# Residual scale and bias as a task beside the gated unit, interleaved GELU, two gates placed anew

## The chip, the cores and the metric

One core of a Trainium2 chip runs the whole program. TensorE (PE) multiplies matrices into PSUM, VectorE (DVE), ScalarE (ACT) and GpSimd (POOL) work on elements, and SyncE (SP) issues every DMA of the kernel in one queue. The engines run side by side, each in its own fixed order, and wait for one another through semaphores. The metric is the device time of one execution in microseconds (us).

## The reference

A decoder trunk of two layers over 528 tokens (16 meta tokens and 512) and 1024 channels. Each layer projects the normalised stream `h`, runs three causal mixers on it (S5, Mamba-2 SSD, gated DeltaNet), merges them with sigmoid gates, projects once more and normalises:

```python
proj = h @ w_in[layer]
# S5 branch, after its scan
v = jax.nn.gelu(y)
v = v * jax.nn.sigmoid(v @ w_glu + b_glu)
y_a = v * jax.nn.silu(z)
...
# merge of the branches and the end of a layer
outs = jnp.einsum('btnw,nwd->btnd', branches, w_branch[layer])
gates = jax.nn.sigmoid(gate_logits.reshape(bsz, t, N_BRANCH, D_MODEL) + b_gate[layer])
merged = jnp.sum(gates * outs, axis=2)
h = _layer_norm(ALPHA * h + merged @ w_out[layer], ln_g[layer], ln_b[layer])
```

## The kernel before

**Products.** All large products are made in float32 precision from two parts. A weight tile `wr` comes by DMA (four buffers), ACT rounds 128 x 256 of it into `wh`, and DVE or POOL computes the rest, `wl = wr - wh`. Such a split of a weight feeds twelve matmuls on PE: three products (`hTh,wh`, `hTl,wh`, `hTh,wl`), two blocks of 128 rows of the weight, two blocks of 264 tokens. `pj` is the PSUM tile of a product, in two buffers.

**Order.** A layer is a list of items that run one after the other: `Gemm` (a product), `Start` (start a task), `Need` (finish a task first), `Back` (read a kept gate back), `OutProj`, and a few more. Smaller work is written as tasks, Python generators, of which `pump()` runs the next piece whenever a product has passed a split. When a piece may run is decided while the program is built, by a planner: the class `Clock` keeps a modelled time for each engine, for every buffer's last write and read, and for the DMA queue. A bare `yield` lets the task go on when its inputs are done by the model, `yield LEAD` somewhat earlier than the model's end of the last operation. `tte` gives an operation to DVE or POOL, whichever is done earlier by the model. So a change of a cost in `Clock` alters the order of instructions on all engines, and nothing else. On the chip each engine then keeps the order that was fixed.

**The places in a layer.** After the S5, SSD and DeltaNet tasks and the merge of branch 2 (`merge_all(2, ...)`) the task `v` applies the GELU to S5's output in two halves: `yc` is loaded from DRAM (`dys`, written with another layout), `gl` is the tanh argument, `vhi` and `vlo` the two parts of the result. Meanwhile PE does the kept gates (`KEPT`: products of gates of branch 0, done early, stored to DRAM in `dgate`) and the merge of branch 1. `Need v` stands before the six GLU products (`w_glu`, about 707 to 736 us in layer 0, 1545 to 1572 in layer 1), then come the six products for S5's gate path z (to 773 and 1606), then the merge of branch 0 (to 811 and 1643), whose gates come back through `Back` (`gth<-dgate`), and then the output projection in four quarters of 256 columns (`OutProj`, to 876 and 1697). In layer 0 the task `s5p1`, the S5 parameters of layer 1 (tiles `s5t`, `s5f`), is started before the GLU products too.

**The residual.** `hdram[l]` holds the normalised stream before its scale and bias. `o_pre` loads its tiles of 128 tokens into `zt` (and the rows of scale and bias into `res`); each quarter of `OutProj` multiplies and adds these for its 256 columns, adds the products (`wo` in PSUM) and takes the statistics (`lnst`) for the next norm. The 16-token tile of layer 0 takes a path of its own (`few_products`).

**The inversion.** DeltaNet's triangular systems are solved in blocks: DVE forms `UL` by products `pr`, `UL` goes to DRAM (`dU`) and comes back transposed (`Ub`), DVE transposes it into `tb`, and PE multiplies (`y<-tb,N`). There are four such places, two for each layer.

## Time and profile before

| What | Value |
| --- | --- |
| Runs (us) | 1722.65, 1719.12, 1711.24; median 1719.12 |
| Profiled execution (us) | 1713.22 |
| Its span in the trace (us) | 1711.5 |
| PE busy | 1619.9 us, 95% |
| DVE busy | 1302.4 us, 76% |
| ACT busy | 821.2 us, 48% |
| POOL busy | 196.4 us, 11% |

The span is the time from the first to the last recorded instruction of the profiled execution. Busy times are sums over the span, so an engine with 76% may be full in one stage and idle in another. All instructions carry line 229, the helper that issues them, so they are told apart by tiles: `wl<-wr,wh` is the operation that reads `wr` and `wh` and writes `wl`.

### The profile page before, as it was taken

To read this page: it belongs to the slowest core of one execution; us is meant where nothing else is said; L and a number is where in the kernel's file an instruction comes from. 1 tells how busy PE (TensorE), PEld (TensorE's weight loads), DVE (VectorE), ACT (ScalarE), POOL (GpSimd) and SP (SyncE) were. 2 spreads that over 40 slices of the span, in tenths; PEclk is the share of its full clock that TensorE was granted. 3 is DMA by queue.
4 is the path that set the end of the run, shared out by engine and by line. 5 is a ranking of instruction groups with operands and counts; after the bars stand their busy time and mean duration, and the time that the engine had idled before them with its cause. 6 is when DMAs were issued, how large, how long until landed. Compare 5 with 4: busy or idle time off the path is not lost.

```text
span 1711.5 us, 40925 instructions
## 1 busy us (share of the span) xinstructions
PE 1619.9 (95%) x15583; PEld 1546.9 (90%) x15583; DVE 1302.4 (76%) x3413; ACT 821.2 (48%) x2057; POOL 196.4 (11%) x352
## 2 busy tenths in 40 slices
PE   6899999999999999999889999999999999999996
PEld 5889999998889899999789999999989999999986
DVE  6897879779868775775767686888888687756676
ACT  5356554347834343443155655444566344344432
POOL 4000000201001000001530000002001000000043
PEclk9999999999999999999999998999999999999998
DMA  5223322252245234336232233232512453443551
GB/s 180 71 81 91 99 72 54 95 115 61 58 105 119 78 114 119 101 92 203 65 119 87 76 98 90 60 85 82 108 54 64 129 103 99 119 130 97 159 168 69
DMA packets 160149, 169.72 MB, mean 99 GB/s; under 512 B 67344, under 2 KB 98192, under 8 KB 159952
## 3 DMA queue, kind: packets, MB, share of 16 engines
q1 hardware_dynamic: 159952, 167.10, 35.1%
q8 instruction: 123, 2.02, 0.5%
q14 instruction: 74, 0.61, 0.1%
HBM read 144.40 MB, written 22.64 MB: 98 GB/s over the span
## 4 chain that ended last, share of the span: by engine, by line
PE 72%; DVE 15%; DMA 6%; issue 3%; ACT 2%; SPq 2%; POOL 0%; DVEq 0%; POOLq 0%; ACTq 0%
PE pj L229 52%; PE wo L229 4%; DVE wl L229 3%; PE y L229 2%; SPq L229 2%; DMA dU<-UL 2%; PE Y L229 2%; PE seg L229 1%; PE o L229 1%; DVE s5t L229 1%; DMA gth<-dgate 1%; DVE pr L229 1%; DVE zt L229 1%; DMA yc<-dys 1%; PE z L229 1%
## 5 line engine op out<-in xcount | busy, mean ns | idle before, releaser
L229 PE MATMUL pj<-hTh,wh 128*128 128x264 f32 (+1 forms) x2432 | 521.8, 295 | 2.0 <-ACT wh L229 2.0
L229 PE MATMUL pj<-hTh,wl 128*128 128x264 f32 (+1 forms) x2432 | 498.6, 285 | 11.4 <-DVE wl L229 11.1
L229 PE MATMUL pj<-hTl,wh 128*128 128x264 f32 (+1 forms) x2432 | 498.6, 286 | 0.0
L229 ACT ACTIVATE wh<-wr 128x256 fp32r<-128x256 f32 x820 | 325.5, 413 | 265.5 <-PE pj L229 214.1
L229 DVE TENSOR_TENSOR wl<-wr,wh 128x256 fp32r<-128x256 f32 x749 | 315.1, 435 | 168.1 <-ACT wh L229 161.5
L229 PEld LDWEIGHTS pj<-hTh,wl 128*128 128x128 f32 x2432 | 380.5, 190 | 15.7 <-DVE wl L229 15.4
L229 PEld LDWEIGHTS pj<-hTh,wh 128*128 128x128 f32 x2432 | 379.0, 191 | 9.4 <-issue 3.5
L229 PEld LDWEIGHTS pj<-hTl,wh 128*128 128x128 f32 x2432 | 382.0, 190 | 0.0
L229 POOL TENSOR_TENSOR wl<-wr,wh 128x256 fp32r<-128x256 f32 x71 | 62.0, 874 | 882.6 <-ACT wh L229 714.2
L229 PE MATMUL pj<-yhi,wh 128*128 128x264 f32 (+1 forms) x576 | 120.2, 290 | 11.9 <-ACT wh L229 5.6
L229 PE MATMUL pj<-yhi,wl 128*128 128x264 f32 (+1 forms) x576 | 117.5, 286 | 3.4 <-DVE wl L229 3.4
L229 PE MATMUL pj<-ylo,wh 128*128 128x264 f32 (+1 forms) x576 | 117.5, 286 | 0.3 <-DVE ylo L229 0.3
L229 PEld LDWEIGHTS pj<-yhi,wh 128*128 128x128 f32 x576 | 90.0, 192 | 14.4 <-issue 6.0
L229 PEld LDWEIGHTS pj<-yhi,wl 128*128 128x128 f32 x576 | 90.2, 191 | 3.9 <-DVE wl L229 3.9
L229 PEld LDWEIGHTS pj<-ylo,wh 128*128 128x128 f32 x576 | 90.6, 192 | 0.8 <-DVE ylo L229 0.8
L229 ACT ACTIVATE craw<-pj 128x528 f32<-128x528 f32 x56 | 34.0, 607 | 54.6 <-PE pj L229 37.3
L229 PE MATMUL wo<-wo,mhi 128*128 128x256 f32 x256 | 51.8, 298 | 2.4 <-DVE wo L229 1.9
L229 ACT ACTIVATE segr<-triu,sc_ghi 128x128 fp32r<-128x128 f32 (+1 forms) x168 | 52.3, 375 | 2.9 <-PE sS L229 2.8
L229 ACT ACTIVATE segr<-triu,sc_glo 128x128 fp32r<-128x128 f32 (+1 forms) x168 | 52.2, 374 | 0.0
L229 ACT ACTIVATE gth<-pj,pars 128x528 f32<-128x528 f32 (+1 forms) x48 | 33.0, 688 | 28.4 <-PE pj L229 28.4
L229 PEld LDWEIGHTS wo<-wo,mhi 128*128 128x128 f32 x256 | 42.2, 201 | 4.9 <-DVE wo L229 2.9
L229 DVE TENSOR_TENSOR s5w<-s5w,s5w 128x132 f32<-128x132 f32 (+1 forms) x144 | 43.1, 313 | 2.9
(384 smaller groups left out, 2776.4 us busy)
## 6 DMA issues: line engine op xcount, KB each, us to landing
wr<-in_w_main_dram SPq DMA_DIRECT2D x304, 256.0 KB
wr<-in_w_branch_dram SPq DMA_DIRECT2D x48, 256.0 KB
wr<-in_w_out_dram SPq DMA_DIRECT2D x32, 256.0 KB
s5t<-dK SPq DMA_DIRECT2D x192, 32.0 KB
wr<-in_w_branch_dram SPq DMA_DIRECT2D x48, 128.0 KB
zt<-hdram SPq DMA_DIRECT2D x8, 512.0 KB
dus<-us SPq DMA_DIRECT2D x12, 264.0 KB
ub<-dus SPq DMA_DIRECT2D x32, 99.0 KB
```

Of the source, the lines that this page charges most:

```text
L229: r = f(*args, **kw)
```

## The change

1. `Clock`: a DMA whose contiguous run is under 256 bytes ends 1900 ns after its bytes have moved by the model, before 650. This concerns the small DMAs of the inversion.
2. `head_scalars` and `s5_bc` get two and three more points at which other work may be put between their operations (`yield LEAD`).
3. `s5_gelu` takes both halves in one task: both `yc` loads are issued first, and the first part of a row's work (square to tanh) runs ahead of the second part of the row before. The tanh rows use the buffers `craw`.
4. The gate of (0,0) is read back ahead of the last z product, and of the last four kept gates one, (0,1), is made after the merge of branch 1.
5. The residual's scale and bias become a task `residual`, started after `Need v`: it loads a tile of `hdram` into `zr` (two buffers `nu`), does the multiplication and the addition in two halves of 512 columns, and stores it back; `OutProj` loads the finished tile. `Need res` stands before `o_pre`. In the order that results, all 20 operations of layer 0 and 16 of layer 1 are on DVE.

```diff
--- before.py
+++ after.py
@@ -193,7 +193,7 @@
             for s in out.shape:
                 size *= s
             self.moved = max(self.q + 650, self.moved) + size / (360.0 if run >= 512 else 180.0)
-            end = self.moved + 650
+            end = self.moved + (1900 if run < 256 else 650)
         else:
             end = t + self.cost(e, op, out, ins, kw)
             self.t[e] = end
@@ -743,8 +743,10 @@
         act(eg, ac[:, :, 0:6], AF.Exp)
         dt8 = small([P, NC, 12], "sc_dt", bufs=1)
         ts(V, dt8, u[:, :, 6:18], 0.125, MUL)
+        yield LEAD
         ts(V, beta, beta, 1.0, ADD)
         V.reciprocal(out=beta, in_=beta)
+        yield LEAD
         glo = small(sh, "sc_glo", bufs=1)
         tt(V, glo, g, f32(ghi), SUB)
         hs.update(dt8=dt8, beta=beta, g=(f32(ghi), glo), te=te, et=et, eg=eg)
@@ -1446,10 +1448,13 @@
         u = t2("su")
         tte(y, b, kk("kr"), MUL)
         tte(u, bx, kk("kis"), MUL)
+        yield LEAD
         tte(y, y, u, ADD)
         tte(yx, bx, kk("krs"), MUL)
+        yield LEAD
         tte(b, b, kk("ki"), MUL)
         tte(yx, yx, b, SUB)
+        yield LEAD
         ts(V, c[64:128], c[64:128], -1.0, MUL)
         w["b"] = dict(y=y, yx=yx, c=c, cx=cx)
         yield
@@ -1580,23 +1585,37 @@
             DMA.dma_start(out=dst[:, :, 7 - i, :], in_=ys[16 * i:16 * i + 16])
         st["yd"] = d
 
-    def s5_gelu(st):
-
-        yc = big("yc")
-        DMA.dma_start(out=yc, in_=st["yd"].rearrange("(a g) c i n -> (g c) a (i n)", a=3))
-        hi, lo = st["v"] = (big("vhi", F32R), big("vlo", F32R))
-        yield
-        for i in range(3):
-            x = yc[:, i, :]
-            t = row("gl")
+    def s5_gelu(sts):
+
+        ycs = [big("yc") for _ in sts]
+        for st, yc in zip(sts, ycs):
+            DMA.dma_start(out=yc, in_=st["yd"].rearrange("(a g) c i n -> (g c) a (i n)", a=3))
+        yield
+
+        def first(x):
+            t = rot(sp, [P, T + 3], F32, "craw", "gl", 2)[:, 0:T]
             act(t, x, AF.Square)
             ts(V, t, t, 0.044715, MUL, 1.0, ADD)
             tte(t, t, x, MUL)
             act(t, t, AF.Tanh, scale=GELU_C)
-            yield
+            return t
+
+        def second(x, t, hi, lo, i):
             stt(x, t, 1.0, x, ADD, MUL)
             hilo_row(x, hi, lo, i, 0)
-            yield
+
+        left = None
+        for st, yc in zip(sts, ycs):
+            for i in range(3):
+                t = first(yc[:, i, :])
+                yield LEAD
+                if left:
+                    second(*left)
+                    yield LEAD
+                if i == 0:
+                    st["v"] = (big("vhi", F32R), big("vlo", F32R))
+                left = (yc[:, i, :], t, *st["v"], i)
+        second(*left)
 
 
     lnc = const([P, DEPTH, 2 * KD], F32, "lnc")
@@ -1828,6 +1847,8 @@
             g, o = zip(*[merge(n, d, xs) for d in range(d0, d1)])
 
             def gate_item(d):
+                if (n, d0 + d) == (0, 0):
+                    return
                 if (n, d0 + d) in kept:
                     items.append(Back(KEPT.index((n, d0 + d))))
                 else:
@@ -1885,12 +1906,32 @@
                 zt[c] = nu("zt") if c < 2 else tok_tile("zt")
                 DMA.dma_start(out=zt[c][:n], in_=hdram[l][t0:t0 + n, :])
                 zt["st", c] = small([P, 4, 6], "lnst", bufs=5)
-            if 0 in which:
-                zt["in"] = [row_vec(A["ln_in" + k] if l == 0 else A["ln" + k][l - 1:l, :],
-                                    flat(sp.tile([P, 2, T], F32, tag="bc", name=nm("res"), bufs=2))[:, 0:D])
-                            for k in ("_g", "_b")]
-            elif lastl:
+            if lastl and 0 not in which:
                 zt["gb"], zt["bb"] = (row_vec(A[k][l:l + 1, :], tok_tile(k)) for k in ("ln_g", "ln_b"))
+
+        def residual():
+
+            rows = [row_vec(A["ln_in" + k] if l == 0 else A["ln" + k][l - 1:l, :],
+                            flat(sp.tile([P, 2, T], F32, tag="bc", name=nm("res"), bufs=2))[:, 0:D])
+                    for k in ("_g", "_b")]
+            zs = {}
+
+            def load(c):
+                t0, n = cs[c]
+                zs[c] = nu("zr")
+                DMA.dma_start(out=zs[c][:n], in_=hdram[l][t0:t0 + n, :])
+
+            load(0)
+            for c in cs:
+                t0, n = cs[c]
+                if c + 1 < len(cs):
+                    load(c + 1)
+                yield
+                for x, op in zip(rows, (MUL, ADD)):
+                    for h in (slice(0, 512), slice(512, D)):
+                        tte(zs[c][:n, h], zs[c][:n, h], x[:n, h], op)
+                        yield LEAD
+                DMA.dma_start(out=hdram[l][t0:t0 + n, :], in_=zs[c][:n])
 
         def last(c):
             return lambda: last_task(zt[c], *cs[c], zt["st", c], zt["gb"], zt["bb"])
@@ -1954,14 +1995,11 @@
                     products(1, range(KD - 1))
                 for c in seq:
                     t0, n = cs[c]
-
-                    zh = zt[c][:n, 256 * qn:256 * qn + 256]
-                    for x, op in zip(zt["in"], (MUL, ADD)):
-                        tte(zh, zh, x[:n, 256 * qn:256 * qn + 256], op)
                     if n < 32:
                         few_products(c)
                     else:
                         products(c, range(KD - 1 if qn == 0 and c < 2 else 0, KD))
+                    zh = zt[c][:n, 256 * qn:256 * qn + 256]
                     stt(zh, zh, ALPHA, ps[c][:n], MUL, ADD)
                     if n < 32:
                         for i in (32, 64, 96):
@@ -2028,22 +2066,23 @@
         items.append(Start("sp" + L, lambda: ssd_post(l, hs, sd, to)))
         merge_all(2, xc, 6, 8)
         items.append(Mark("xc" + L))
-        def f_v():
-            for hf in range(2):
-                yield from s5_gelu(s5[hf])
-
-        items.append(Start("v" + L, f_v, "fB" + L, "sp" + L))
+        items.append(Start("v" + L, lambda: s5_gelu(s5), "fB" + L, "sp" + L))
+        keep_gates(3)
+        merge_all(1, xb, 0, 8, "sp" + L)
+
         keep_gates(len(KEPT) - len(kept))
-        merge_all(1, xb, 0, 8, "sp" + L)
-
         items.append(Need("v" + L))
+        items.append(Start("res" + L, residual))
         if not lastl:
             items.append(Start(f"s5p{l + 1}", lambda: s5_params(l + 1)))
         for o in range(6):
             items.append(Gemm(A["w_glu"][l, o], 6, vx, FULL, c_glu(o)))
         items.append(Do(lambda: None))
         for o in range(6):
+            if o == 5:
+                items.append(Back(KEPT.index((0, 0))))
             main(CT_ZA + o, c_za(o), blocks)
+        items.append(Need("res" + L))
         items.append(Do(lambda: o_pre((0, 1))))
         merge_all(0, xa, 0, 8)
         items.append(Do(lambda: None))
```

Three places show how the order of instructions moves. DVE's order in the first inversion of layer 0, before, up to the transpose `tb` (`x` and `g_r` are other work of the same task):

```order
L229 TENSOR_TENSOR wl_3028<-wr_2732,wh_3027 128x256
L229 TENSOR_TENSOR g_rt_3009<-g_r_3008 128x30
L229 SCALAR_TENSOR_TENSOR g_rt_3009<-g_rt_3009,g_x_2710 128x30
L229 SCALAR_TENSOR_TENSOR g_r_3008<-g_rt_3009,g_r_3008 128x30
L229 TENSOR_TENSOR wl_3047<-wr_2732,wh_3046 128x256
L229 SCALAR_TENSOR_TENSOR x_2771<-craw_2963,pars,x_2771 128x528
L229 COPY N_1858<-Ub_2890 32x12x32 x2
L229 STREAM_TRANSPOSE tb_3063<-Ub_2890 128x384
L229 TENSOR_SCALAR g_r_3008<-g_r_3008 128x30
```

The same place in the changed order:

```order
L229 CAST r_556_3084<-rest_557_3086 128x5x3
L229 TENSOR_TENSOR r_556_3084<-rest_557_3086,r_556_3084 128x5x3
L229 TENSOR_TENSOR wl_3103<-wr_2772,wh_3102 128x256
L229 TENSOR_TENSOR wl_3123<-wr_2892,wh_3122 128x256
L229 SCALAR_TENSOR_TENSOR x_2762<-cth_3120,x_2762 128x528
L229 TENSOR_TENSOR wl_3140<-wr_2892,wh_3139 128x256
L229 SCALAR_TENSOR_TENSOR x_2762<-craw_3097,pars,x_2762 128x528 x2
L229 COPY N_1912<-Ub_2939 32x12x32 x2
L229 STREAM_TRANSPOSE tb_3185<-Ub_2939 128x384
L229 TENSOR_TENSOR wl_3188<-wr_2972,wh_3187 128x256
```

Counted from the last product `UL<-UL,pr`, six `wl` stood ahead of `tb` and nine stand there now.

ACT's order at the GELU of layer 0, from the copy `ys` whose store completes `dys`, before:

```order
L229 ACTIVATE ys_8329<-Y_9865 128x264
L229 ACTIVATE wh_9903<-wr_9669 128x256
L229 ACTIVATE wh_9921<-wr_9732 128x256
L229 ACTIVATE gth_9939<-pj_9836,pars 128x528
L229 ACTIVATE wh_9942<-wr_9775 128x256
L229 ACTIVATE wh_9958<-wr_9775 128x256
L229 ACTIVATE wh_9976<-wr_9841 128x256
L229 ACTIVATE wh_9994<-wr_9841 128x256
L229 ACTIVATE gl_10012<-yc_9893 128x528
L229 ACTIVATE gl_10012<-gl_10012 128x528
L229 ACTIVATE wh_10017<-wr_9907 128x256
L229 ACTIVATE wh_10033<-wr_9907 128x256
```

The same place in the changed order:

```order
L229 ACTIVATE ys_8329<-Y_9867 128x264
L229 ACTIVATE wh_9904<-wr_9733 128x256
L229 ACTIVATE wh_9922<-wr_9733 128x256
L229 ACTIVATE wh_9940<-wr_9774 128x256
L229 ACTIVATE wh_9956<-wr_9774 128x256
L229 ACTIVATE wh_9974<-wr_9822 128x256
L229 ACTIVATE gth_9992<-pj_9921,pars 128x528
L229 ACTIVATE wh_9995<-wr_9859 128x256
L229 ACTIVATE wh_10011<-wr_9859 128x256
L229 ACTIVATE wh_10029<-wr_9926 128x256
L229 ACTIVATE gl_10039<-yc_9894 128x528
L229 ACTIVATE gl_10039<-gl_10039 128x528
```

Six `wh` stood between `ys` and the first `gl`, eight stand there now; `wr_9926` of the eighth is requested on SP behind both loads of `yc`. Behind these rows there is one `wh` and then a second pair of `gl`; before, two `wh` followed the pair.

SP's order at the end of the z products of layer 0, before:

```order
L229 DMA wr_11488<-in_w_branch_dram 128x512
L229 DMA wr_11506<-in_w_branch_dram 128x256
L229 DMA zt_11526<-hdram_85 128x1024
L229 DMA zt_11529<-hdram_85 128x1024
L229 DMA res_11532<-in_ln_in_g_dram 128x1024
L229 DMA res_11534<-in_ln_in_b_dram 128x1024
L229 DMA gth_11536<-dgate_87 128x528
L229 DMA gth_11538<-dgate_87 128x528
L229 DMA wr_11561<-in_w_branch_dram 128x512
```

The same place in the changed order:

```order
L229 DMA hdram_85<-zr_10912 128x1024
L229 DMA zr_11357<-hdram_85 16x1024
L229 DMA wr_11363<-in_w_branch_dram 128x512
L229 DMA wr_11405<-in_w_branch_dram 128x256
L229 DMA wr_11442<-in_w_branch_dram 128x512
L229 DMA hdram_85<-zr_11189 128x1024
L229 DMA gth_11481<-dgate_87 128x528
L229 DMA wr_11488<-in_w_branch_dram 128x256
L229 DMA wr_11526<-in_w_branch_dram 128x512
L229 DMA hdram_85<-zr_11357 16x1024
L229 DMA wr_11545<-in_w_branch_dram 128x256
L229 DMA zt_11567<-hdram_85 128x1024
```

The `res` rows have left this place, the first `gth` stands ahead of the reloads of `zt`, and the stores `hdram<-zr` with the loads behind them are new; a load of `zr` waits until the store from the same buffer is done. The second `zt` and the second `gth` follow these rows. In layer 0 there are three loads that wait for a store in this way, in layer 1 two.

## Rows read from the trace of the kernel before

**Rows 1.** The page: span, busy time of each engine, its share and instructions.

```profile
span 1711.5 us, 40925 instructions
...
PE 1619.9 (95%) x15583; PEld 1546.9 (90%) x15583; DVE 1302.4 (76%) x3413; ACT 821.2 (48%) x2057; POOL 196.4 (11%) x352
```

**Rows 2.** The waits of PE over the whole span: sum, times, longest.

```profile
PE pj L229 <- DVE wl L229: 16.2, 16, 2.4
...
PE pj L229 <- ACT wh L229: 7.6, 5, 3.0
PE wo L229 <- DVE wl L229: 6.2, 11, 1.9
PE pj L229 <- DVE gth L229: 4.7, 2, 2.4
...
PE y L229 <- DVE tb L229: 2.6, 2, 2.0
PE y L229 <- DVE go_f L229: 2.0, 1, 2.0
PE wo L229 <- DVE wo L229: 1.9, 5, 0.9
...
PE y L229 <- DVE g_r L229: 1.1, 1, 1.1
```

**Rows 3.** Windows: length, each engine's busy time (instructions), PEclk, DMA share, GB/s.

```profile
301.90:305.20 3.30, 3.30 (x26) 3.21 (x23) 2.10 (x5) 2.02 (x6) 0.00 (x0) 0.50 0.93 294
513.50:516.80 3.30, 3.30 (x17) 3.30 (x16) 2.71 (x18) 0.67 (x2) 0.52 (x1) 0.50 0.74 234
667.10:670.40 3.30, 3.30 (x17) 3.30 (x16) 2.35 (x6) 2.69 (x6) 0.00 (x0) 0.50 0.34 92
830.90:834.30 3.40, 3.05 (x14) 3.05 (x15) 1.15 (x3) 0.00 (x0) 0.00 (x0) 0.50 0.02 5
...
1052.80:1059.60 6.80, 6.80 (x62) 6.74 (x59) 5.96 (x12) 5.12 (x19) 0.10 (x1) 0.50 0.36 128
...
1660.40:1667.10 6.70, 5.42 (x25) 5.13 (x25) 4.90 (x9) 0.00 (x0) 6.16 (x8) 0.50 0.37 120
```

**Rows 4.** The chain, 190 to 208 us: start, length, what.

```profile
194.37 7.51 DMA dU<-UL
...
203.36 1.96 DMA Ub<-dU
...
205.99 1.58 PE y L229 x48
```

**Rows 5.** The chain, 770 to 790 us.

```profile
774.88 8.63 DMA gth<-dgate
```

**Rows 6.** Groups of DVE, 815.1 to 830.8 us (first quarter of OutProj, layer 0).

```profile
L229 DVE TENSOR_TENSOR wl<-wr,wh 128x256 fp32r<-128x256 f32 x5 | 3.9, 818 | 0.0
```

**Rows 7.** Groups of DVE, 849 to 865 us (last quarters of OutProj).

```profile
L229 DVE TENSOR_TENSOR wl<-wr,wh 128x256 fp32r<-128x256 f32 x4 | 1.5, 416 | 0.0
```

**Rows 8.** Groups of POOL, 815.1 to 865 us.

```profile
L229 POOL TENSOR_TENSOR zt<-zt,res 128x256 f32<-128x256 f32 x21 | 16.6, 801 | 0.7
```

**Rows 9.** Timeline of ACT, 655 to 668 us: start, length, operation, idle before.

```profile
662.65 0.64 ACT L229 ACTIVATE gl<-yc 128x528 f32<-128x528 f32 x1 [5.39 <-DMA yc<-dys]
...
665.08 0.70 ACT L229 ACTIVATE wh<-wr 128x256 fp32r<-128x256 f32 x2
```

**Rows 10.** Windows of the GLU and z products, and of one load of `yc`.

```profile
721.00:736.00 15.00, 14.21 (x112) 13.57 (x111) 14.66 (x64) 5.54 (x13) 0.00 (x0) 1.00 0.30 96
...
1572.00:1606.00 34.00, 34.00 (x290) 34.00 (x289) 21.45 (x40) 15.44 (x35) 0.00 (x0) 1.00 0.27 79
...
686.00:688.50 2.50, 2.50 (x23) 2.50 (x22) 0.43 (x1) 1.07 (x3) 0.00 (x0) 1.00 0.98 365
```

**Rows 11.** Groups of DVE, 706 to 773 us.

```profile
L229 DVE TENSOR_TENSOR acc<-acc,gth 128x528 f32<-128x528 f32 x2 | 1.4, 706 | 0.0
```

**Rows 12.** The waits of SP's queue over the whole span.

```profile
SPq L229 <- DMA dU<-UL: 20.3, 4, 5.1
```

## Prediction

> **What bounds the kernel now.** I read the page first: TensorE (PE) is busy for 1619.9 of 1711.5 us, VectorE (DVE) for 1302.4, GpSimd (POOL) for 196.4 [rows 1]. PE sets the end, so the change can win only what PE loses, and I looked for that loss in two places. The first is the view of PE's waits [rows 2]: the reader is to see that the named waits are short and many, and that each belongs to a place which the change touches. Pieces of weights not yet split by DVE (`pj<-wl`) cost 16.2 us; in the output projection `wl` and `wo` cost 6.2 + 1.9; the gate read back from DRAM (`gth`) 4.7 in two waits; the inversion (`y`) 2.6 + 2.0 + 1.1; and ScalarE's casts (`wh`, mostly the two behind the GELU) 7.6. The second loss is the granted clock: in some stretches it is 0.50 instead of 1.00, that is 1.2 instead of 2.4 GHz [rows 3]. Ahead of each of these stands a wait of PE. A stretch at half clock loses half of PE's busy time in it: 3.30 us cost 1.65, the pieces of 6.8 us cost 2.7 to 3.4.
>
> One more number is needed throughout. PE did 290 matmuls in the 34.00 us from 1572 [rows 10], 0.117 us each. One split of a weight (`wh` with its `wl`, 128 x 256) feeds twelve, so a split is 1.41 us of cover for PE. In the output projection one split feeds three, 0.35 us.
>
> **Part 1: later results of small DMAs in the planner (the inversion).** No instruction is added; the planner believes that short-run transfers end later, and so orders what uses them later. The chain [rows 4] shows `dU<-UL` 7.51 us, then `Ub<-dU` 1.96, then `tb`, then `y` on PE: from `dU`'s start to `y` 205.99 - 194.37 = 11.6 us. Between the last product of the inversion and `tb`, DVE's order had six splits and has nine (the four places: 6, 9, 7, 8 before and 9, 11, 8, 11 now). Six are 8.5 us of cover for 11.6, nine are 12.7: in that place `y` should no longer wait. At the place with only one split more, some wait stays. What can be won is 5.7 us of waits [rows 2] plus the half-clock stretches behind them, two of 3.3 us (one stands, 301.90) and one of 6.8 (1052.80) [rows 3]: 2 x 1.65 + 3.4 = 6.7; together 12.4. I take **10**, since one place gains only 1.41 of cover. Ends: 3 (the chain has more DVE work in front of `tb` and grows with the cover) and 12.4. The wait of DVE for `Ub` is covered by the splits made ahead of it.
>
> **Part 2: yields in the head scalars and the S5 B/C maps.** Seven `smap` operations ran in a row ahead of the next split; now splits may stand between them. The wait there is at most 2.4 (the longest of `pj<-wl`) [rows 2], with a half-clock stretch behind it (513.50) [rows 3], 1.65. The weights themselves come late there too, so I take half of 4.05, **2**; ends 0 and 4, or -2 when the maps become late for their readers.
>
> **Part 3: the GELU of both halves as one interleaved task.** Before, ACT waits 5.39 us for `yc<-dys` (one stands; layer 1 repeats it), with the next weight's cast queued behind it on ACT, and PE dries out [rows 9]: `pj<-wh` 7.6 in all [rows 2], and a half-clock stretch (667.10, and again in layer 1) [rows 3]. The excerpt of ACT's order shows what changes: eight casts instead of six stand between `ys` and the first `gl`, of which one comes from a tile that SP now requests behind **both** loads of `yc`. For the second load the nearest row is the stretch in which it ran alone: 686.00 to 688.50 at 365 GB/s [rows 10], so 792 KB take 2.2 us more ahead of that weight. Then the two `gl` pairs have only one cast between them; a pair holds ACT from 662.65 until the next cast at 665.08 [rows 9], 2.4 us, against 1.41 of cover: 1.0 short. Per layer: +2.2 + 1.0 - 1.4 (one split more of cover that is truly there) = 1.8 worse, so **3.6 lost**; the half-clock stretch stays. Ends: a gain of 4 (both extra splits cover) and a loss of 8.
>
> **Part 4: the gate (0,0) loaded earlier, one store of a gate later.** The chain shows 8.63 us from the issue of `gth<-dgate` to its landing, at 774.88 [rows 5], because two `zt`, two `res` and two tiles of weights (over 2 MB) are ahead of it on SP. In the changed order its load stands ahead of the last z weights, and the `res` rows are gone from this place. Both waits of `gth`, 4.7 us [rows 2], should go; no half-clock stretch follows them. I take **4.5**; ends 3 and 4.7. What could be late next is the second gate, now behind the reloads of `zt`; its gate is wanted three splits (4.2 us) later than the first, which covers the reloads of 1 MB at 365 GB/s (2.9 us). The product of gate (0,1) that moves behind the second merge takes PE as long as before, and nobody waits for its store.
>
> **Part 5: the residual's scale and bias as a task.** It leaves the output projection: 40 operations in layer 0 (29 on POOL) and 32 in layer 1 (17 on POOL). There DVE's `wl` takes 818 ns beside POOL's `zt<-zt,res` of 801, and 416 in the later quarters, when POOL is idle [rows 6 to 8]. PE asks for a split every 0.35 us there, so 818 starves it and 416 nearly keeps up, given the tiles split ahead. What is lost there: waits 6.2 + 1.9 = 8.1 [rows 2], and half-clock stretches of PE busy 3.05 (twice, one stands, 830.90) and 5.42 (1660.40) [rows 3], half of which is 1.5 + 1.5 + 2.7 = 5.7. Of these 13.8 I take **12**: the last of a quarter's sums and statistics still stand ahead of the next quarter's splits on DVE. Ends 6 (POOL gets splits instead, and DVE is slowed by those) and 13.8. The Trainium skill ("SBUF — State Buffer", section "Who interferes with whom") says that a DVE operation with two SBUF inputs and a GpSimd operation that reads SBUF share a port pair as an exclusive lock, and that the loser fully blocks. The trace agrees in kind (416 against 818 ns); one split passes per POOL operation. By that rule alone nothing of the 818 would remain without POOL's work, and the sum would have 13.8 in place of 12.
>
> It returns beside the GLU and z products, all on DVE. The price is that of a like operation there, `acc<-acc,gth` of 706 ns for 528 columns [rows 11]; for 512 it is 0.68, times 20 in layer 0 is 13.7 us and times 16 in layer 1 is 10.9. In layer 0 DVE was busy 14.66 of 15 us from 721 to 736 [rows 10], since the next layer's S5 parameters run there as well; with the task, DVE's demand reaches PE's time through this stage, so that a lag of a few us must show. I take **3.5** lost (ends 0 and 10). In layer 1 DVE was busy 21.45 of 34 us [rows 10], and 10.9 fits into the slack: **1** lost (ends 0 and 4).
>
> SP's queue gets store-then-load pairs: a `zr` load waits until the store from its buffer is done, and weights are queued behind it; three in layer 0, two in layer 1. The nearest row is `dU<-UL`: four waits of SP, 20.3 us, the longest 5.1 [rows 12]; I take 5.1 for these larger stores, 2.0 as the lower end (the shortest landing in [rows 4]). The cover is the tiles already loaded, six splits or 8.5 us, so I cost it at 0; without cover it would be 3 x 5.1 + 2 x 5.1 = 25.5. The Trainium skill ("DMA: Bandwidth & Descriptors", section "Anatomy of one DMA") speaks against such pairs: a transfer has some 2 us of fixed cost, most of it the write's receipt, and most for HBM. By it five waits would hold SP for at least 10 us; no row here shows a store of 512 KB alone.
>
> **The sum.** 10 + 2 - 3.6 + 4.5 + 12 - 3.5 - 1 = 20.4 us less. The profiled execution took 1713.2 us, which would become 1692.8. The median of the runs, 1719.1, lies 5.9 above it and the runs spread from 1711.2 to 1722.7; the median would become 1698.7, and I predict **1699**.
>
> **Rivals.**
> *DVE takes it back.* The inversion gives its lower end 3, the output projection 8, the gate 4, part 2 nothing; the GELU loses 7, DVE in layer 0 lags 10 and in layer 1 3. That is 15 - 20 = 5 slower, 1724, within 1%; halfway to it is 1711. For it speaks the 14.66 of 15 us [rows 10]; against it, that the planner may give splits to POOL there, and that PE has splits in store. About 17 us, 1%, is what a measurement of this kernel tells from no change.
> *SP becomes the bound.* From the point at which a store holds SP longer than the 8.5 us of splits in store, each of the five pairs dries PE out. At 5.1 us of wait with no cover this is 25.5, and a half-clock stretch behind each 5 x 1.65 = 8.3; with the second `yc` load ahead of weights the GELU loses 8. Against 28.5 of gains and 4.5 of DVE's lag this ends at 25.5 + 8.3 + 8 + 4.5 - 28.5 = 18 slower, 1737. Against it speaks that SP waits for `wl` most of the time anyway, so weights are well ahead.
> *The inversion does not change.* If DVE reaches `tb` later by as much as the cover grew, part 1 gives 0 and the rest stands: 1709.
>
> **How the numbers follow.** The forecast (1685 to 1702) has 0.52, DVE takes it back wholly or in part 0.27, the unchanged inversion 0.13, SP 0.08. Of the forecast's cases nearly all are faster by over 1% (below 1702), and a little of the two middle ones: 0.56. Slower by over 1% (above 1736) are most of SP's cases, 0.07. The range reaches from 1682 (the output projection and the inversion at their upper ends and a GELU that gains) to 1722, which takes in most of the middle cases.
>
> **What would show it.** In the profile after: `y` waits under 1.5 us in all; no `gth` wait; in the output projection `wl` near 0.42 us, POOL almost idle and PE's waits under 3 us; a `wh` wait behind `gl` that stays at 2.5 to 4 us in each layer; some `wl` waits between 706 and 773. The prediction is wrong if the inversion's waits only move, if the GLU and z products of layer 0 take over 8 us more than 66, or if waits for weights appear behind `hdram<-zr`.

## The result and the profile after

The changed kernel took 1695.72 us at the median (four runs, 1693.98 to 1700.20), the kernel before 1715.70 in the same comparison. The ratio is 0.9887, 95% interval 0.9858 to 0.9917: 1.1% faster. The profiled execution went from 1713.22 to 1693.98 us, its span from 1711.5 to 1692.3. Forecast were 20.4 us less; measured are 19.2 there, and 20.0 by the medians. Each profile below is of one execution; that of the changed kernel is the fastest of its four.

The page and the view of PE's waits after the change (columns as in [rows 1, 2]):

```profile
span 1692.3 us, 40917 instructions
...
PE 1612.4 (95%) x15583; PEld 1536.3 (91%) x15583; DVE 1294.5 (76%) x3416; ACT 820.3 (48%) x2057; POOL 169.1 (10%) x313
```

```profile
PE pj L229 <- DVE wl L229: 16.8, 18, 4.6
PE pj L229 <- ACT wh L229: 12.9, 10, 2.8
...
PE bc L229 <- ACT N L229: 3.0, 2, 1.9
...
PE pj L229 <- ACT vhi L229: 1.5, 2, 1.0
PE pj L229 <- ACT yhi L229: 1.4, 1, 1.4
```

Against [rows 2] the reader is to see three groups gone: `gth`, `wo<-wl` and `wo<-wo`, and the waits of `y`. One has grown by 5.3 (`wh`), three are new (`bc<-N`, `vhi`, `yhi`), and `wl` is as large as before, so its waits must stand elsewhere now. Lengths of the stages show where, taken from the first matmul of each stage in either trace:

| Stage | before (us) | after (us) | difference |
| --- | --- | --- | --- |
| start to GLU, layer 0 | 706.7 | 707.4 | +0.7 |
| GLU and z products, layer 0 | 66.1 | 72.1 | +6.0 |
| last merge, layer 0 | 37.9 | 38.1 | +0.2 |
| output projection, layer 0 | 65.3 | 54.2 | -11.1 |
| to GLU, layer 1 | 669.2 | 662.3 | -6.9 |
| GLU and z products, layer 1 | 60.7 | 64.5 | +3.8 |
| last merge, layer 1 | 37.1 | 34.4 | -2.7 |
| output projection, layer 1 | 54.2 | 46.5 | -7.7 |
| rest | 14.3 | 12.8 | -1.5 |

Windows of the profile after (columns as in [rows 3]):

```profile
722.00:737.00 15.00, 12.32 (x97) 11.68 (x96) 14.59 (x56) 4.90 (x12) 0.77 (x1) 1.00 0.29 80
737.00:756.00 19.00, 14.41 (x106) 14.20 (x105) 18.65 (x79) 4.54 (x11) 0.73 (x1) 0.91 0.41 141
756.00:780.00 24.00, 23.80 (x195) 23.59 (x195) 23.19 (x45) 10.15 (x24) 2.61 (x3) 1.00 0.46 151
...
817.00:872.00 55.00, 53.12 (x474) 49.46 (x472) 38.00 (x98) 18.85 (x46) 9.96 (x14) 1.00 0.35 116
229.20:232.50 3.30, 3.30 (x20) 3.18 (x19) 1.81 (x4) 1.88 (x4) 0.95 (x1) 0.50 0.08 13
1058.60:1065.30 6.70, 5.57 (x30) 4.64 (x29) 3.90 (x10) 4.68 (x13) 0.00 (x0) 0.50 0.12 40
748.00:751.30 3.30, 3.30 (x17) 3.30 (x16) 3.13 (x15) 1.11 (x3) 0.73 (x1) 0.50 0.32 96
```

DVE is busy 18.65 of 19 us in the z products and PE only 14.41: there the bound has changed hands, with a half-clock stretch behind it (748.00). In the output projection PE is busy 53.12 of 55 us at full clock. One half-clock stretch stands behind the longer of the two new waits of `bc` (229.20). Another (1058.60) lies around the shorter one, but it began 1.3 us before that wait did.

### The profile page after: what moved, and what is told of

It is laid out like the page before. It is cut to its first block, busy times and chain, and to the rows that moved or that the text cites. A ratio compares the mean times of both kernels' runs of the same rounds, so it can differ in the third digit from the quotient of the medians.

```text
span 1692.3 us, 40917 instructions
## 1 busy us (share of the span) xinstructions
PE 1612.4 (95%) x15583; PEld 1536.3 (91%) x15583; DVE 1294.5 (76%) x3416; ACT 820.3 (48%) x2057; POOL 169.1 (10%) x313
## 4 chain that ended last, share of the span: by engine, by line
PE 74%; DVE 14%; ACT 3%; DMA 3%; issue 3%; SPq 2%; POOL 1%; POOLq 0%; DVEq 0%; ACTq 0%
PE pj L229 54%; PE wo L229 4%; DVE wl L229 2%; PE y L229 2%; SPq L229 2%; PE Y L229 1%; DMA wr<-in_w_main_dram 1%; PE seg L229 1%; PE o L229 1%; DVE s5t L229 1%; DVE x L229 1%; ACT wh L229 1%; PE V L229 1%; PE z L229 1%; DVE pr L229 1%
## 5 line engine op out<-in xcount | busy, mean ns | idle before, releaser
L229 PE MATMUL pj<-hTh,wl 128*128 128x264 f32 (+1 forms) x2432 | 497.8, 285 | 13.6 <-DVE wl L229 13.4
L229 DVE TENSOR_TENSOR wl<-wr,wh 128x256 fp32r<-128x256 f32 x740 | 302.9, 425 | 188.4 <-ACT wh L229 185.5
L229 PEld LDWEIGHTS pj<-hTh,wl 128*128 128x128 f32 x2432 | 379.0, 190 | 18.4 <-DVE wl L229 18.2
L229 POOL TENSOR_TENSOR wl<-wr,wh 128x256 fp32r<-128x256 f32 x80 | 69.9, 874 | 943.3 <-ACT wh L229 770.1
L229 PE MATMUL wo<-wo,mhi 128*128 128x256 f32 x256 | 47.3, 282 | 0.4 <-DVE gth L229 0.2
```

What stands on the lines that cost most here:

```text
L229: r = f(*args, **kw)
```

## The experiments

Every kernel here computes the whole reference. Times are medians; the changed kernel's is 1695.7, that of before 1715.7 to 1720.2 in the four comparisons. A distance in us from the changed kernel crosses comparisons: 1715.7 was measured for before beside the changed kernel and 2 to 4.5 us more beside the experiments, so by the ratios these distances come out some 2 to 5 us lower. The first three runs undo one part of the change each.

**Part 1 undone.**

```diff
-            end = self.moved + (1900 if run < 256 else 650)
+            end = self.moved + 650
```

> The changed kernel with part 1 alone undone (650 ns for all DMAs in the planner). Theory (cover): the splits again stand too few between the last product of an inversion and its transposed reload, so waits of y on PE come back, 4 to 6 us in all, with half-clock stretches behind them; the time is 8 to 12 us above the changed kernel. Rival (any new order would do): the y waits stay below 1.5 us in all, or come back without the total moving by more than 3 us.

Measured: 1709.4 us, ratio to before 0.9945 [0.9910, 0.9980], 13.7 above the changed kernel. PE's waits:

```profile
PE pj L229 <- ACT wh L229: 21.5, 9, 4.9
...
PE y L229 <- DVE tb L229: 4.2, 3, 1.8
...
PE y L229 <- DVE go_ft L229: 1.8, 1, 1.8
```

The `y` waits are back, 6.0 us. In exchange the waits of `bc` for `N`, 3.0 us in the changed kernel, are gone. Both hold in the other runs: the five kernels with 650 ns wait 5.3 to 6.2 us ahead of `y` and never for `N`; the nine with 1900 ns all wait for `N`, 1.9 to 4.0 us, and ahead of `y` in one only (the lead of 1400 ns below, 4.3). So part 1 acts at its own place, but about half of the wait moves on to the next link of the inversion. And these waits are less than half of the 13.7: `wh` has grown by 8.6, mostly in waits at 517, 728 and 1359 us, none of them at an inversion. A second thing moves the total.

**Part 5 undone:** the task `residual`, its `Start` and its `Need` are taken out, and the two `tte` of each quarter put back into `OutProj`.

> The changed kernel with part 5 alone undone (scale and bias back in the output projection). Theory: the output projection takes 62 to 66 us in layer 0 instead of 54, and some 8 us more in layer 1, with POOL's 0.80 us operations beside splits of over 0.7 us; the GLU and z products of layer 0 get 5 to 6 us shorter, those of layer 1 up to 3; the total is 10 to 14 us above the changed kernel. Rival (DVE's load is only moved from one stage to the other): the total stays within 3 us.

Measured: 1710.9 us, ratio 0.9954 [0.9933, 0.9975], 15.2 above. The output projection takes 66.1 and 53.8 us. PE's waits, the groups of DVE and of POOL from 812 to 878 us:

```profile
PE wo L229 <- DVE wl L229: 5.9, 10, 1.9
...
PE wo L229 <- DVE wo L229: 2.0, 5, 1.0
```

```profile
L229 DVE TENSOR_TENSOR wl<-wr,wh 128x256 fp32r<-128x256 f32 x13 | 9.1, 734 | 0.0
```

```profile
L229 POOL TENSOR_TENSOR zt<-zt,res 128x256 f32<-128x256 f32 x23 | 18.0, 795 | 0.8
```

The rows of [rows 2, 6, 8] come back in kind. GLU and z products of layer 0 take 67.7 us, 4.4 less than with the task; in layer 1, 63.2, 1.3 less. The rival falls by these stages: 19.2 us lost in the output projection against 5.7 won. By the total alone it would not, since the lead of 1400 ns below moves the total as far with a new order only.

**Part 3 undone:** `s5_gelu` for one half after the other, as before.

> The changed kernel with part 3 alone undone (the two halves of the GELU one after the other, each with its own load of yc). Theory: the weight that stood behind both loads of yc is there 2 us earlier, ACT's casts wait less, and the total is 2 to 6 us below the changed kernel. Rival (the interleaving earns its keep, since the first gl comes after eight splits instead of six): the total is 2 to 4 us above.

Measured: 1701.2 us, 5.5 above the changed kernel (1 by the ratios), ratio 0.9894 [0.9861, 0.9926]. The theory expected it below. PE's waits for `wh` are 17.1 and for `vhi` 3.7 (12.9 and 1.5 after). No gain of the old order shows; by what follows next, 5.5 us are within what an order alone can do, so neither side is shown.

**A new order and nothing else.**

```diff
-            t[1] = ... clock.end + (-1500.0 if r is LEAD else Clock.HOP)
+            t[1] = ... clock.end + (-1400.0 if r is LEAD else Clock.HOP)
```

> The changed kernel with only the planner's lead of a task changed from 1500 to 1400 ns; no work is added, removed or moved on purpose. It measures what a new order alone does to the time. Theory (the parts act at their own places): the total stays within 4 us of the changed kernel. Rival (all differences of this size are luck of the order): it moves by 8 us or more.

Measured: 1710.1 us, 14.4 above, ratio 0.9945 [0.9919, 0.9971]. The theory fell, and this was the run that mattered most. The chain around the second inversion of layer 1 shows one of the places:

```profile
1150.51 0.47 SPq L229
...
1151.08 3.10 DMA wr<-in_w_main_dram
...
1154.28 0.42 ACT wh L229
...
1155.08 0.34 DVE N L229
...
1155.83 0.59 DVE tb L229
...
1156.56 1.45 PE y L229 x27
```

SP's and DVE's timelines there:

```profile
1139.89 3.63 SPq L229 DMA_DIRECT2D dU<-UL  x2
1148.60 1.87 SPq L229 DMA_DIRECT2D Ub<-dU  x4
...
1151.08 0.37 SPq L229 DMA_DIRECT2D wr<-in_w_main_dram  x1
```

```profile
1154.73 0.43 DVE L229 TENSOR_TENSOR wl<-wr,wh 128x256 fp32r<-128x256 f32 x1 [3.94 <-ACT wh L229]
...
1155.83 0.58 DVE L229 STREAM_TRANSPOSE tb<-Ub 128x384 f32<-128x384 f32 x1
```

SP issued the two `dU<-UL` from 1139.89 on, then held its queue until the store was done and issued `Ub<-dU` at 1148.60; the next weight stood behind these and started at 1151.08. DVE's order has that weight's split ahead of `tb`, so `y` waited 3.3 us, with the planner's 1900 ns in place. So I ran three more draws of an order: the kernel before at 1400 and 1600 ns, and the changed one at 1600, each with the same one-line edit.

> The kernel before with the planner's lead at 1400 instead of 1500 ns. Theory (output projection and gates give the change its fixed gain of some 20 to 25 us, which the new order partly gives back or not): this stays within 6 us of before, since waits before were not those of a lucky order, and its output projection stays at 65 and 54 us. Rival (the total is mostly luck of the order): it moves by 8 us or more, either way, and may come out as fast as the changed kernel.

> The kernel before with the lead at 1600 ns: a second draw of an order for the old program. Theory: within 6 us of before. Rival: it moves by 8 us or more.

> The changed kernel with the lead at 1600 ns: a third draw for the new program, after 1500 and 1400. Theory: the output projection again takes 54 and 46 us, no gth wait; the total lies between 1695 and 1712. Rival (1500 was the lucky one and the change itself is worth nothing): 1712 or more.

| Lead in the planner | before (us) | changed (us) |
| --- | --- | --- |
| 1400 ns | 1711.9 | 1710.1 |
| 1500 ns | 1715.7 to 1720.2 | 1695.7 |
| 1600 ns | 1728.0 | 1709.6 |

Ratios to before: 0.9962 [0.9938, 0.9986] and 1.0053 [1.0032, 1.0075] for the old program, 0.9939 [0.9918, 0.9960] for the new one at 1600. The means of the ratios are 1.0005 and 0.9924 (0.9887, 0.9945, 0.9939). By them the change is worth an estimated 0.8%, 14 us, and the order that came with 1500 ns gave some 6 more; with three orders on each side the standard error of the 14 is 5.5 us. All three new draws lie below all three old ones, the nearest pair 1.8 us apart. Neither expectation of the two runs of the old program stands whole: it moved by 8 both ways. The third draw of the new one came as expected, and its three lie 14 us apart (10 by the ratios). The gain in the output projection does not move with the order. In every kernel with the residual's work inside the output projection by `tte`, this takes 64.5 to 66.1 and 53.8 to 54.2 us; in every kernel that has the task and starts nothing else there, 54.2 to 55.3 and 45.7 to 46.9. PE's waits for DVE's `gth` are 4.1 to 4.6 us in the two new draws of before, and no product `pj` waits for it in the changed kernels. What does move is the price beside it: GLU and z products of layer 0 take 72.1, 70.4 and 78.8 us in the three changed kernels (leads of 1500, 1400, 1600), 66.0 to 66.6 in the three old ones.

**What made the output projection slow.** The kernel before, with all 72 operations on DVE:

```diff
-                        tte(zh, zh, x[:n, 256 * qn:256 * qn + 256], op)
+                        tt(V, zh, zh, x[:n, 256 * qn:256 * qn + 256], op)
```

> The kernel before with all operations of the residual's scale and bias given to DVE in the output projection, so that POOL does none of them. Theory (splits starve because POOL's operations slow DVE's): wl takes 0.42 us in every quarter; DVE does 29 and 17 operations of 0.42 more, 12 and 7 us, and the output projection gets 3 to 8 us shorter in layer 0 than 65, not all the 11. Rival (it was DVE's own load): wl at 0.42 but the output projection stays at 65 us or grows.

Measured: 1707.2 us, ratio 0.9936 [0.9910, 0.9962]; the output projection takes 60.8 and 49.1. Groups of DVE from 810 to 880 us, and PE's waits:

```profile
L229 DVE TENSOR_TENSOR zt<-zt,res 128x256 f32<-128x256 f32 x32 | 13.8, 431 | 0.6
L229 DVE TENSOR_TENSOR wl<-wr,wh 128x256 fp32r<-128x256 f32 x19 | 7.6, 439 | 1.0 <-ACT wh L229 1.0
```

```profile
PE wo L229 <- DVE wl L229: 5.3, 6, 1.2
```

With POOL out of the way a split takes 439 ns beside more work on DVE, and 4.5 + 5.1 = 9.6 us are won. The task won 18.8. So about half of that came with taking POOL's 46 operations away, and the other half with taking all 72 out of the stage. The Trainium skill ("SBUF — State Buffer", section "Who interferes with whom") names the pair of ports. The trace agrees that both engines slow each other: in the kernel before, a split took 419 ns with POOL idle (mean of 658) and 838 inside POOL's work (mean of 12); POOL's `zt<-zt,res` took 735 ns with DVE idle (two of 46) and 831 inside DVE's work (mean of 33). The price here: moving 46 operations from POOL to the busier engine made the stage shorter. In total this one line, with one order drawn, reaches 0.9936; that is not told apart from the 0.9924 of the whole change.

**The GELU's second load.**

```diff
+            if st is sts[0] and i == 0:
+                load(1)
```

behind the first `gl` pair, in place of the second `yc` load at the start.

> The changed kernel with the second load of yc issued after the first gl pair of the first half instead of right behind the first load. Theory: the weight behind the loads arrives 2 us earlier and the first gl too; waits for wh at the GELU of both layers shrink from 3.8 and 4.7 us to under 3 each. The stage from there to the output projection is shorter by 2 to 4 us in each layer. Rival (the wait is for the first load and the strided stores ahead of it): the wh wait at the first gl stays at 2.8 us or more; the total stays within 4 us, order aside.

Measured: 1693.3 us, ratio 0.9863 [0.9819, 0.9908], not to be told from the changed kernel. ACT's timelines of the changed kernel and of this one:

```profile
657.30 0.42 ACT L229 ACTIVATE wh<-wr 128x256 fp32r<-128x256 f32 x1 [0.20 <-PE pj L229]
665.65 0.42 ACT L229 ACTIVATE wh<-wr 128x256 fp32r<-128x256 f32 x1 [7.93 <-DMA wr<-in_w_main_dram]
665.97 0.63 ACT L229 ACTIVATE gl<-yc 128x528 f32<-128x528 f32 x1
```

```profile
661.57 0.41 ACT L229 ACTIVATE wh<-wr 128x256 fp32r<-128x256 f32 x1
667.10 0.64 ACT L229 ACTIVATE gl<-yc 128x528 f32<-128x528 f32 x1 [5.12 <-DMA yc<-dys]
```

In the changed kernel ACT does wait for the weight behind both loads, as forecast. With the load moved `gl` starts 5.5 instead of 8.7 us after the cast ahead of it, but PE's wait in this stretch only goes from 3.5 to 3.2 us, and in layer 1 from 4.2 to 3.7 (before: 2.6 and 3.0). The rival was right in its first half: what PE waits for is the first load, which SP issued behind the eight strided stores of `ys`; that the stores make it late was not tested.

This kernel has the changed kernel's order up to the GELU, and yet its profiled execution came to the GLU products at 712.3 us instead of 707.4, with 4.9 us of difference there before the GELU. Two pairs of profiles of one order show what such a difference is made of. Here it is mostly the stretch behind the wait of `bc` near 227 us (1.88 us in the changed kernel, 2.19 in this one), at full clock in the first row and at half clock in the second:

```profile
232.50:242.40 9.90, 9.32 (x88) 7.99 (x88) 7.87 (x15) 4.53 (x12) 0.77 (x3) 1.00 0.20 64
228.80:242.40 13.60, 13.02 (x77) 11.46 (x75) 6.67 (x12) 5.80 (x15) 1.72 (x4) 0.50 0.11 34
```

The kernel before and the run with all 72 operations on DVE have one order up to the output projection. Both wait for `y` near 300 us, 1.97 and 1.99 us. In the first the half clock ends after 3.3 us (301.90 in [rows 3], and the first row here), in the second it lasts 20.4:

```profile
305.30:320.20 14.90, 14.90 (x196) 13.53 (x196) 7.71 (x17) 5.20 (x12) 2.88 (x5) 1.00 0.34 112
299.80:320.20 20.40, 20.40 (x199) 18.90 (x196) 6.65 (x15) 6.26 (x15) 2.77 (x5) 0.50 0.38 129
```

So a wait of the same length can cost very different stretches of half clock, and what one profile shows of them is one draw.

**DVE in layer 0's GLU and z products.** Three ways to unload it. First the task later, on top of the edit before:

```diff
         for o in range(6):
             items.append(Gemm(A["w_glu"][l, o], 6, vx, FULL, c_glu(o)))
+        items.append(Start("res" + L, residual))
...
-        merge_all(0, xa, 0, 8)
+        merge_all(0, xa, 4, 8)
```

with `merge_all(0, xa, 0, 4)` ahead of `Need res` and `o_pre`.

> As the kernel before this one, and the residual task starts after the GLU products and is needed in the middle of the last merge, so that it does not run beside the next layer's S5 parameters. Theory (DVE is full in layer 0's GLU and z products because both tasks are there): GLU and z products of layer 0 take 67 us or less instead of 72, waits for wl between 707 and 780 under 3 us; the total is 3 to 8 us below the kernel before this one. Rival (SP's waits on its stores delay the weights): the waits move with the task to the z products and the merge, and the sum of the three stages stays at 108 to 110 us.

Measured: 1701.6 us, ratio 0.9898 [0.9867, 0.9930], 8.3 above the kernel before this one, where 3 to 8 less were expected. GLU and z products take 67.1 and 60.9 us, 5.3 and 2.9 less than in the kernel before this one, but the last merges 39.2 and 40.5 instead of 36.8 and 34.5. The rows of PE's waits and of the merge of layer 1:

```profile
PE pj L229 <- ACT yhi L229: 4.3, 2, 2.7
```

```profile
1597.00:1637.00 40.00, 37.12 (x287) 36.47 (x286) 26.15 (x51) 15.60 (x37) 4.44 (x6) 0.91 0.61 196
```

What was won ahead of the merges was lost in them, to the parts of the last z row (`yhi`) and a half-clock stretch.

Then on POOL:

```diff
-                        tte(zs[c][:n, h], zs[c][:n, h], x[:n, h], op)
+                        ttg(zs[c][:n, h], zs[c][:n, h], x[:n, h], op)
```

> The changed kernel with the residual task's operations on POOL instead of DVE. Theory (what costs is DVE's full time there): DVE gets 13.7 us free in layer 0, but its two-input operations beside POOL's slow down, splits to 0.6 us or more; in the GLU and z products of layer 0 the gain and the loss about cancel, 68 to 74 us. Rival (the lock takes all): DVE operations wait for POOL's of 1.5 us in full and the stage takes over 76 us.

Measured: 1708.2 us, ratio 0.9936 [0.9910, 0.9963]. Groups of POOL and DVE, 707 to 780 us:

```profile
L229 POOL TENSOR_TENSOR zr<-zr,res 128x512 f32<-128x512 f32 x11 | 17.8, 1645 | 13.4 <-DMA zr<-hdram 13.4
```

```profile
L229 DVE TENSOR_TENSOR wl<-wr,wh 128x256 fp32r<-128x256 f32 x39 | 17.7, 465 | 10.5 <-ACT wh L229 10.5
```

GLU and z products take 72.4 us, within the 68 to 74 expected, but splits take 465 ns and not 600: POOL works on only part of the stretch, as it waits 13.4 us for `zr`. It ran late instead, and the last merge took 45.6 us.

Last, the next layer's S5 parameters ahead of the output projection instead of the GLU products, on top of the later second load:

> As e9, and the next layer's S5 parameters start ahead of the output projection instead of ahead of the GLU products (layer 0 only). Theory: GLU and z products of layer 0 take 67 us or less; the output projection of layer 0, where DVE has time now, stays below 58; the total is 4 to 8 us below e9. Rival (DVE is full there too, or the parameters are late for layer 1): the output projection grows by what the GLU stage gains.

Measured: 1698.9 us, ratio 0.9888 [0.9843, 0.9932]. GLU and z products take 68.8, the output projection 68.0. PE's waits and the window of the output projection:

```profile
PE wo L229 <- issue: 5.3, 1, 5.3
```

```profile
815.00:883.00 68.00, 56.87 (x467) 51.99 (x466) 53.64 (x204) 18.89 (x46) 11.89 (x15) 0.92 0.30 94
```

The rival was right: the output projection grew by 13.7, almost four times what the GLU stage gained (72.4 in the kernel without this edit). The total is 5.6 us above its base, where 4 to 8 less were expected; that is within the scatter of orders. None of these versions is shown to be faster than the changed kernel.

## Why the prediction was right

The total, the range and the sign held: 20.4 us less forecast, 19.2 measured, 1695.7 in 1682 to 1722. That the total came so near is in part luck. The other two orders of the same change, 1710.1 and 1709.6, lie in the range too, but not in the forecast's 1685 to 1702; they lie at the rival that gives the inversion nothing, 1709. The stages of the three profiles on each side, both layers together, show where the sum was off:

| Stages | forecast (us) | before, mean of three orders | changed, mean of three orders | difference |
| --- | --- | --- | --- | --- |
| up to the GLU products | -8.4 | 1379.0 | 1380.0 | +1.0 |
| GLU and z products | +4.5 | 126.7 | 139.0 | +12.3 |
| last merges | -4.5 | 75.8 | 72.9 | -2.9 |
| output projections | -12 | 119.0 | 100.6 | -18.4 |
| rest | 0 | 14.4 | 12.6 | -1.8 |

In the first row the three orders of either program lie 16 to 17 us apart, so this row tells no difference, neither +1.0 nor the forecast; in the second and the fourth the programs do not overlap. Inside the sum, then, two clear errors cancelled, a larger gain and a larger price, and a third term is not confirmed.

**The output projection** was under-sized: 12 forecast, ends 6 and 13.8, measured 18.8. Windows of the two projections, before and then after:

```profile
810.70:876.00 65.30, 57.68 (x468) 52.25 (x467) 49.10 (x109) 18.79 (x46) 30.12 (x39) 0.95 0.29 95
1643.00:1697.20 54.20, 49.97 (x386) 48.04 (x384) 38.34 (x80) 13.39 (x31) 20.58 (x26) 0.94 0.27 92
817.60:871.80 54.20, 52.32 (x468) 48.80 (x467) 37.27 (x97) 18.85 (x46) 9.84 (x13) 1.00 0.35 114
1633.00:1679.50 46.50, 46.11 (x386) 45.36 (x384) 26.80 (x68) 13.55 (x31) 9.65 (x13) 1.00 0.32 111
```

For the same number of matmuls PE is idle 9.6 us less and busy 9.2 us less. The sum had 8.1 of named waits and 5.7 of half clock, and took these as all that could be won; 1.5 of idle and 3.5 of busy time go beyond that, and for the 3.5 no row has a name. The mechanism, splits slowed by POOL, is shown for about half of the gain; the other half came with all 72 operations leaving. One reading was too strong: a split every 0.35 us is asked for only while PE passes over the first block of tokens of a quarter. The same split serves the later blocks, so that in layer 0 some 33 splits stand beside 384 matmuls of `wo`.

**The return beside the GLU and z products** was under-sized as well: 3.5 and 1 forecast, 6.0 and 3.8 measured in these stages, and 12.3 together in the mean of three orders. With a lead of 1600 ns layer 0's took 78.8, beyond the 8 us over 66 that the prediction had named as a sign of being wrong. That DVE is full in layer 0 is shown: 18.65 of 19 us busy, the longest wait of `wl` 4.6, and 5.3 us less with the task moved on. Not all of the loss is the task's: with part 5 undone the stages were only 4.4 and 1.3 shorter. So that 10.9 us would nearly fit into layer 1's slack held in that pair, 1 forecast and 1.3 measured; the other 2.5 there stand without the task, and waits for `vhi`, 1.5 us, show that the GELU ended late.

**SP's stores ahead of loads** stayed covered as forecast. In the waits of SP's queue:

```profile
SPq L229 <- DMA hdram<-zr: 17.8, 6, 4.5
```

Five of the six are the expected loads of `zr`, 2.3 to 4.5 us each and 3.3 on the average (2.0 to 5.1 were the bounds); the sixth, 1.2, stands behind the store of the 16-token tile. All lie under the 8.5 us of splits in store, and no wait of PE was traced to them. The Trainium skill ("DMA: Bandwidth & Descriptors", section "Anatomy of one DMA") has some 2 us of fixed cost, measured on DMAs that GpSimd issues. Here SP issues them, and the five waits of 2.3 us and more are not below that figure.

**The gates** went as forecast: `gth` no longer waits; 4.5 forecast of 4.7. In layer 0 waits of `yhi`, 1.4, and of `wl`, 0.7, took the place, so that this merge did not get shorter; both merges together gave 2.5.

**The inversion, the yields and the GELU** together: 10 + 2 - 3.6 = 8.4 forecast, and the stages up to the GLU products gave 6.9 - 0.7 = 6.2, nearly all in layer 1; over three orders, the first row of the table, nothing of it can be told from the scatter. The `y` waits went, and with part 1 undone they were back at 6.0; but in every kernel with part 1 waits of `bc` for `N` took their place, 3.0 us here, in layer 0 with a half-clock stretch behind. So what the prediction had called a sign of being wrong, that the inversion's waits only move, came about in half. I had asked what is late next only for splits, not for the inverse's next link. That the GELU's weight stands behind both loads was right; that it is what PE waits for was not.

**What the prediction lacked** is the order itself. It costed each part at its place, as if the rest of the schedule stood still. With its two neighbouring leads the old program spreads over 16 us and the new one over 14, so an estimated 6 of the 20 us are this order's, and not the change's. Both slower profiles of the new program lose 5 to 6 us ahead of layer 0's GLU products and nearly 10 ahead of layer 1's. Which of the many moved instructions make that luck stays open: only the place at 1150 us was followed.

## What to carry to other kernels

Before crediting a change in a program whose order a planner fixes, shift a planner constant that does no work, in both versions: the scatter of those runs is the error bar, and here it was as large as the effect. Compare the versions stage by stage over the same shifts: where the lengths of a stage do not overlap, as in the output projection here, a few runs tell what a total cannot. Work on a second engine is not free because that engine idles: price it by what the critical engine's operations take beside it, and compare with doing it on the critical engine. When work leaves a stage, look in the stage that receives it at the busy time of the receiving engine for each stretch, not for the whole span.

## What the runs showed of the hardware that was not expected

One DVE split of 128 x 256 took 416 ns alone, 465 ns beside POOL operations on 512 columns that ran part of the time, and 734 to 818 ns beside a dense run of POOL operations on 256 columns, which themselves took 0.80 us (0.74 with DVE idle). A store of 512 KB held the queue's next load into the same buffer for 3.3 us on the average of five. Two executions of one order of instructions were 4.9 us apart before the middle of the program, mostly because behind the same wait, 1.9 and 2.2 us, TensorE's clock stood at 1.2 GHz for 3.3 us in one and 13.6 in the other; in a second pair it was 3.3 and 20.4.
